# A two-layer streaming encoder: where the entry of gate and up keeps its norm scales, its rounded parts and its PSUM banks

## The chip, the core and the metric

The kernel runs on one core of one Trainium2 chip. The metric is the device time of one execution in microseconds, the median of several runs.

## The reference, cut to what matters

Two request groups (1024 prompt frames, and 8 x 16 sample frames) go through two trunk layers with width 1024. Each layer is a mixer with a residual and then a gated feed-forward block with a residual:

```python
h = rmsnorm(x, norm_mix[layer])
x = x + mixer(h)                    # layer 0: S5 + gated DeltaNet, then @ w_out; layer 1: windowed attention, then @ wo
x = x + swiglu(rmsnorm(x, norm_ffn[layer]), w_gate, w_up, w_down)

def rmsnorm(x, w):  y = x * rsqrt(mean(x * x) + 1e-6);  return y * w
def swiglu(h, w_gate, w_up, w_down):  return (silu(h @ w_gate) * (h @ w_up)) @ w_down
```

All is fp32. The change sits where each layer passes from the projection (`@ w_out` or `@ wo`) to the norm and to the products with `w_gate` and `w_up`.

## The kernel before, in words

The activations stand transposed: `x` is 8 chunks of 128 channels by 1152 frames, and the frames are cut in 3 blocks of 384 (`BW`). A product in fp32 is made of three matmuls on fp32r values (`mm3`, lines 436 to 438): each operand is split into a rounded part (`hi`, a ScalarE copy) and a remainder (`lo`, source minus `hi`, on VectorE).

`project` makes the projection. In its second half it goes over blocks and chunks; each of the 24 results is accumulated in one of two PSUM banks (`bank`), VectorE adds it into `x` (line 1509), ScalarE squares it (line 341), GpSimd adds up the squares (line 347), and after the eighth chunk of a block `rms` (lines 349 to 364) sums them over the partitions with matmuls into a bank `pn` and makes the scale 1/rms of the block in an SBUF tile `r`.

`ffn` follows. `scale` (line 478) multiplies the eight chunks of a block by the norm's weight and by the block's scale: 8 VectorE instructions, one block at a time, 24 for a layer. Gate and up are made by a fast algorithm of 20 products (`UP_A`, `UP_ORDER`) whose right operands are sums of quarters of the three blocks. `put` (lines 464 to 469) splits one such operand of 128 x 768: one ScalarE instruction for `hi`, one VectorE instruction for `lo`; 20 for a layer. The output tiles `f` = 0 and 1 (`g0`, `g1`) are worked on in turns while the operands are being made; tiles 2 to 21 follow with all operands ready. `weights` sums the weight quarters on GpSimd (line 518) and splits them (lines 522 and 523). Accumulators of `tile_of` go round `banks`: here one `bank` (2 buffers) and three `pa` (6 buffers), eight PSUM banks in all. They are evicted by `copy` (line 549, ScalarE) and `op` (line 555, mostly VectorE).

The order of instructions on each engine is made beforehand by a list scheduler from the order in the program, from priorities (`Sooner` moves evictions and splits forward) and from a model of costs; on the chip each engine goes through its list in order. `mphase` closes a layout of six PSUM banks and opens the next. The six `pa` banks are opened in `ffn`, after the whole projection; the norm sums of the projection use the layout before it.

Of the kernel before, what the change touches and what calls it, by code (L numbers as in the profile page):

```python
# [24 lines left out]
KC = 8  # L25
# [177 lines left out]
def body(tc, nc, I, O):  # L203
# [55 lines left out]

    class Sooner:  # L260
# [88 lines left out]
    def rms(r, b, parts, first=0):  # L349
# [13 lines left out]
        V.scalar_tensor_tensor(y, t, 1.5, y, ALU.add, ALU.mult)  # L363
# [5 lines left out]
    def norm(w, h, r, new, first, keep=None):  # L369
# [4 lines left out]
        def fill(x, k, b, i=None):  # L374
# [4 lines left out]
            if i == KC - 1:  # L379
                rms(r, b, parts, first)  # L380
# [64 lines left out]
    def ffn(x, pre, l, w, nxt):  # L445
        r, hb, c_hb, tp, c_tp, d_r = pre
# [3 lines left out]
        fp, c_fp = po.open(f"fa{l}", side="right")  # L450
        mphase(pa=6)
        banks = itertools.cycle([bank] + [lambda: mbank("pa")] * 3)

        def two(i):
            n = UP_ORDER.index(i)
            pool, tag, bufs = ((hp, "h", 4 * NB), (fp, "u", 4), (hb, "f", 4))[(n >= 12) + (n >= 16)]
# [5 lines left out]
        def put(i, t, neg=False):  # L462
            U[i] = hi, lo = two(i)
            if neg:
                S.activation(hi, t, AF.Copy, scale=-1.0)
                V.scalar_tensor_tensor(lo, t, -1.0, hi, ALU.mult, ALU.subtract)
            else:
                S.copy(hi, t)
                V.tensor_sub(lo, t, hi)  # L469
# [4 lines left out]
        def scale(t, order=range(4)):  # L474
            for q in order:
                for k in (2 * q, 2 * q + 1):
                    o = x[:, k, blk(UP_T[t])]
                    V.scalar_tensor_tensor(o, o, nw[:, w * KC + k:w * KC + k + 1], r[:, blk(UP_T[t])], ALU.mult, ALU.mult)
# [160 lines left out]

        scale(0)  # L640
        b0, b1, b2 = (quarter(t) for t in range(3))
        put(4, b0[3], True)
        put(10, b0[0], True)
        scale(2, (1, 0, 2, 3))
# [4 lines left out]
        V.tensor_add(b2[0], b0[0], b2[0])  # L649
        put(17, b2[0], True)  # L650
# [61 lines left out]
        finishing(g1)  # L712

# [798 lines left out]
    def project(name, ap, x, opnd, view, w, between, places=()):  # L1512
# [23 lines left out]
        between()  # L1536
        wb, c_wb = po.open(name)
# [4 lines left out]
        fill = norm(w, {}, r, lambda: wb.tile([128, BW], F32, name="sq", tag="sq", bufs=3), 0)  # L1542
# [12 lines left out]
        for b in range(NB):  # L1555
            for m in range(KC):
                def ev(b, s, p):
                    add_into(x, m)(b, s, p)
                    if m % 2:
                        Q.dma_start(d_r[m // 2][:, :, s], x.tiles[m // 2][:, :, s])  # L1560
                    fill(x, m, b)
                t = terms(W[m // 2], 512 * (m % 2), 1)
# [422 lines left out]
```

## Time and profile before

| | |
|---|---|
| median of 3 runs | 2755.37 us (2753.17 to 2763.01) |
| profiled execution | 2758.04 us, span 2756.3 us |
| mean granted TensorE clock | 0.960 of full speed |
| busy, share of the span | PE 94%, VectorE (DVE) 72%, ScalarE (ACT) 40%, GpSimd (POOL) 60% |

The span goes from the first to the last instruction. A busy time is the time in which an engine had an instruction in work; two that overlap are counted once. A duration is that of one instruction. A wait in brackets is the idle time of the engine ahead of the instruction, with the one that ended it.

### The profile page before, as it was taken

Reading aid. Unit: us, or ns where it says so; the run is one execution under the profiler, and the core shown is the slowest. Engines: PE = TensorE matmul, PEld = TensorE weight load, DVE = VectorE, ACT = ScalarE, POOL = GpSimd, SP = SyncE. Lnnn points to the kernel's source line nnn. Section 1 sums busy time; section 2 is a strip of 40 time slices with the busy share of each in tenths; the row PEclk is TensorE's granted clock in tenths of the full one; section 3 lists DMA queues with packets and bytes.
Section 4 is the critical chain, followed back from the end, with each engine's and each line's share of the span. In section 5 each row is a group of like instructions: output and inputs, shape, how many; then the busy total and the mean of one; then the engine's idle time right before and its main releaser. Section 6 shows DMA issues by size and latency. Waiting matters only on the chain.

```text
span 2756.3 us, 40229 instructions
## 1 busy us (share of the span) xinstructions
PE 2587.2 (94%) x14777; PEld 2404.8 (87%) x14777; DVE 1997.0 (72%) x3195; ACT 1109.8 (40%) x2232; POOL 1643.3 (60%) x1659
## 2 busy tenths in 40 slices
PE   6898899998799999989999999999789999989996
PEld 5788798997799999989998966667689999989996
DVE  7747874668878777698866245555978777789967
ACT  5234565444344434343333144343334443444332
POOL 8649432226598887897632012113688888788735
PEclk9899999999899999999999999798999999999998
DMA  6432277632022222253313100202122222253311
GB/s 204 134 102 87 95 240 220 189 131 87 33 102 78 91 72 80 79 186 98 98 32 110 61 16 24 86 29 85 33 99 78 77 89 75 74 175 105 100 54 69
DMA packets 164164, 267.20 MB, mean 97 GB/s; under 512 B 34188, under 2 KB 123948, under 8 KB 162928
## 3 DMA queue, kind: packets, MB, share of 16 engines
q1 hardware_dynamic: 163392, 262.28, 29.5%
q8 instruction: 116, 1.90, 0.3%
q10 hardware_dynamic: 576, 2.36, 0.2%
q14 instruction: 80, 0.66, 0.1%
HBM read 186.92 MB, written 79.51 MB: 97 GB/s over the span
## 4 chain that ended last, share of the span: by engine, by line
PE 67%; DVE 13%; POOL 11%; issue 3%; DMA 2%; ACT 2%; SPq 0%; DVEq 0%; POOLq 0%; ACTq 0%
PE pa L436 6%; PE pa L437 6%; PE pa L438 6%; PE pg L307 3%; PE pg L309 3%; PE pg L308 3%; PE pd L438 3%; PE pd L436 3%; PE pd L437 3%; PE b L436 3%; PE b L438 3%; PE b L437 3%; PE pO L1897 3%; PE pS L1870 2%; POOL x L518 2%
## 5 line engine op out<-in xcount | busy, mean ns | idle before, releaser
L436 PE MATMUL pa<-u,whi 128*128 128x384 f32 x928 | 319.6, 344 | 26.5 <-DVE bt L555 13.2
L438 PE MATMUL pa<-u,wlo 128*128 128x384 f32 x928 | 310.3, 344 | 11.3 <-DVE wlo L523 11.3
L437 PE MATMUL pa<-u,whi 128*128 128x384 f32 x928 | 317.2, 342 | 1.5 <-DVE u L469 1.2
L437 PE MATMUL pd<-g,whi 128*128 128x384 f32 x708 | 239.9, 339 | 0.0
L436 PE MATMUL pd<-g,whi 128*128 128x384 f32 x708 | 239.1, 338 | 0.5 <-ACT nt L810 0.5
L438 PE MATMUL pd<-g,wlo 128*128 128x384 f32 x708 | 237.7, 337 | 0.0
L523 DVE TENSOR_TENSOR wlo<-x,whi 128x1024 fp32r<-128x1024 f32 (+2 forms) x176 | 202.7, 1170 | 44.9 <-ACT whi L522 44.5
L522 ACT CAST whi<-x 128x1024 fp32r<-128x1024 f32 (+2 forms) x176 | 129.7, 761 | 256.0 <-PE pa L437 148.6
L1858 POOL TENSOR_SCALAR p<-p,rd 128x192 f32<-128x192 f32 (+3 forms) x80 | 61.3, 768 | 285.7 <-DVE rd L1852 181.0
L518 POOL TENSOR_TENSOR x<-raw 128x256 f32<-128x256 f32 (+1 forms) x230 | 209.9, 936 | 25.7 <-DMA raw<-in_wg_dram 14.7
L436 PEld LDWEIGHTS pa<-u,whi 128*128 128x128 f32 x928 | 178.7, 193 | 32.8 <-DVE bt L555 13.9
L518 POOL TENSOR_TENSOR cm<-raw 128x256 f32<-128x256 f32 (+1 forms) x162 | 158.9, 1002 | 60.3 <-DVE wlo L523 28.0
L438 PEld LDWEIGHTS pa<-u,wlo 128*128 128x128 f32 x928 | 178.7, 193 | 13.6 <-DVE wlo L523 13.6
L284 ACT CAST whi<-raw 128x1024 fp32r<-128x1024 f32 x113 | 116.5, 1049 | 182.7 <-PE pg L308 83.7
L285 DVE TENSOR_TENSOR wlo<-raw,whi 128x1024 fp32r<-128x1024 f32 x113 | 164.6, 1456 | 23.4 <-ACT whi L284 22.7
L437 PEld LDWEIGHTS pa<-u,whi 128*128 128x128 f32 x928 | 178.6, 192 | 2.8 <-DVE u L469 1.7
L436 PE MATMUL pa<-u,x 128*128 128x384 f32 x428 | 146.1, 341 | 4.4 <-DVE bt L555 4.0
L307 PE MATMUL pg<-h0h,whi 128*128 128x384 f32 x384 | 135.0, 352 | 12.1 <-DVE ut L949 11.4
L437 PE MATMUL pa<-u,x 128*128 128x384 f32 x428 | 145.5, 340 | 0.0
L518 POOL TENSOR_TENSOR x<-x 128x256 f32<-128x256 f32 (+1 forms) x142 | 129.2, 930 | 23.1 <-DVE wlo L523 16.4
L438 PE MATMUL pa<-u,x 128*128 128x384 f32 x428 | 141.9, 341 | 0.3
L772 DVE TENSOR_TENSOR g<-gf,g 128x384 fp32r<-128x384 f32 x132 | 135.4, 1052 | 4.3 <-ACT g L771 4.3
(731 smaller groups left out, 8112.6 us busy)
## 6 DMA issues: line engine op xcount, KB each, us to landing
gf<-d_g SPq DMA_DIRECT2D x44, 576.0 KB
raw<-in_wd_dram SPq DMA_DIRECT2D x44, 512.0 KB
raw<-in_wg_dram SPq DMA_DIRECT2D x28, 512.0 KB
raw<-in_wu_dram SPq DMA_DIRECT2D x28, 512.0 KB
raw<-in_win_dram SPq DMA_DIRECT2D x21, 512.0 KB
d_r<-x SPq DMA_DIRECT2D x24, 384.0 KB
x<-d_r SPq DMA_DIRECT2D x8, 1152.0 KB
x<-in_wg_dram SPq DMA_DIRECT2D x16, 512.0 KB
```

Of the source, the lines that this page charges most:

```text
L284: S.copy(hi, raw)
L285: V.tensor_sub(lo, raw, hi)
L307: PE.matmul(p[:, :BW], hi[:, c], rh, start=(i == 0), stop=False)
L308: PE.matmul(p[:, :BW], hi[:, c], rl, start=False, stop=False)
L309: PE.matmul(p[:, :BW], lo[:, c], rh, start=False, stop=(i == len(ks) - 1))
L436: PE.matmul(p, hi[:, c], uh, start=start, stop=False, skip_group_check=more)
L437: PE.matmul(p, hi[:, c], ul, start=False, stop=False, skip_group_check=more)
L438: PE.matmul(p, lo[:, c], uh, start=False, stop=stop, skip_group_check=more)
L518: (P.tensor_add if sg > 0 else P.tensor_sub)(cm[:, 256 * j:256 * (j + n)], fa, ga)
L522: S.copy(hi[:, c], src)
L523: V.tensor_sub(lo[:, c], src, hi[:, c])
L772: eng.tensor_sub(op[1], t, op[0])
```

## The change

Norm scales: `rms` may write the scale of a block into the PSUM bank `pn` that held its sum, and `scale` reads it there. Remainders: `split` takes the place of `put`'s two instructions; ScalarE makes two rounded copies of 128 x 384 in two PSUM banks `ph`, then `hi` of 128 x 768 in SBUF as before, and VectorE makes `lo` in two instructions of 128 x 384, each from the source in SBUF and a rounded copy in PSUM. Banks: one layout for projection and entry, `pn` 1, `ph` 2, `pa` 3, opened ahead of the projection's second half; the products of `f` = 0 and 1 go round five banks, and the six `pa` are opened for `f` = 2 and on. Since one `pn` bank now holds a scale until it is used, `project` becomes a generator, and `ffn` asks for its three blocks between its own first steps.

```diff
--- before.py
+++ after.py
@@ -257,6 +257,19 @@
 
         return behind(S.preload_act_table_set("natural_log_exp_and_others"), *others)
 
+    def split(hi, lo, src, neg=False):
+
+
+        p = [mbank("ph")[:, :BW].bitcast(F32R) for c in range(2)]
+        for c in range(2):
+            S.activation(p[c], src[:, c], AF.Copy, scale=-1.0 if neg else 1.0)
+        S.activation(hi, src, AF.Copy, scale=-1.0 if neg else 1.0)
+        for c in range(2):
+            if neg:
+                V.scalar_tensor_tensor(lo[:, c], src[:, c], -1.0, p[c], ALU.mult, ALU.subtract)
+            else:
+                V.tensor_sub(lo[:, c], src[:, c], p[c])
+
     class Sooner:
 
 
@@ -346,7 +359,8 @@
         else:
             P.tensor_add(ssq[:, s], ssq[:, s], sq)
 
-    def rms(r, b, parts, first=0):
+    def rms(r, b, parts, first=0, banks=None):
+
 
         s = blk(b)
         y, v = r[:, s], ssq[:, s]
@@ -360,13 +374,16 @@
         act.append(S.activation(y, y, AF.Exp, scale=-0.5))
         V.scalar_tensor_tensor(t, y, -0.5, v, ALU.mult, ALU.mult)
         V.tensor_mul(t, t, y)
-        V.scalar_tensor_tensor(y, t, 1.5, y, ALU.add, ALU.mult)
+        o = y
+        if banks is not None:
+            o = banks[b] = p
+        V.scalar_tensor_tensor(o, t, 1.5, y, ALU.add, ALU.mult)
         return act
 
     def new_r():
         return rp.tile([128, T], F32, name="r", tag="r", bufs=1)
 
-    def norm(w, h, r, new, first, keep=None):
+    def norm(w, h, r, new, first, keep=None, banks=None):
 
 
         parts = []
@@ -377,7 +394,7 @@
                 split_in(x, h, w, k, b)
             square_in(x, k, b, i, new, parts, keep)
             if i == KC - 1:
-                rms(r, b, parts, first)
+                rms(r, b, parts, first, banks)
 
         return fill
 
@@ -443,30 +460,26 @@
             pool.tile([128, 1024], F32R, name=t, tag=t, bufs=2)
 
     def ffn(x, pre, l, w, nxt):
-        r, hb, c_hb, tp, c_tp, d_r = pre
+        r, hb, c_hb, tp, c_tp, d_r, project_block, scales = pre
         d_g = dr.tile([NF, 128, T], F32, name=f"d_g{l}")
 
 
-        fp, c_fp = po.open(f"fa{l}", side="right")
-        mphase(pa=6)
-        banks = itertools.cycle([bank] + [lambda: mbank("pa")] * 3)
+        def bp():
+            return mbank("pa")
+
+        banks = itertools.cycle([bank, bp, bank, bp, bp])
 
         def two(i):
             n = UP_ORDER.index(i)
-            pool, tag, bufs = ((hp, "h", 4 * NB), (fp, "u", 4), (hb, "f", 4))[(n >= 12) + (n >= 16)]
+            pool, tag, bufs = (hp, "h", 4 * NB) if n < 12 else (fp, "u", 4) if n < 16 else (hb, "f", 4)
             t = pool.tile([128, 4, BW], F32R, name=f"u{i}", tag=tag, bufs=bufs)
             return t[:, 0:2], t[:, 2:4]
 
         U = {}
 
         def put(i, t, neg=False):
-            U[i] = hi, lo = two(i)
-            if neg:
-                S.activation(hi, t, AF.Copy, scale=-1.0)
-                V.scalar_tensor_tensor(lo, t, -1.0, hi, ALU.mult, ALU.subtract)
-            else:
-                S.copy(hi, t)
-                V.tensor_sub(lo, t, hi)
+            U[i] = two(i)
+            split(*U[i], t, neg)
 
         def quarter(t):
             return [x.tiles[q][:, :, blk(UP_T[t])] for q in range(4)]
@@ -475,7 +488,7 @@
             for q in order:
                 for k in (2 * q, 2 * q + 1):
                     o = x[:, k, blk(UP_T[t])]
-                    V.scalar_tensor_tensor(o, o, nw[:, w * KC + k:w * KC + k + 1], r[:, blk(UP_T[t])], ALU.mult, ALU.mult)
+                    V.scalar_tensor_tensor(o, o, nw[:, w * KC + k:w * KC + k + 1], scales[UP_T[t]], ALU.mult, ALU.mult)
 
         def some(name="bt", bufs=2):
             return tp.tile([128, 2, BW], F32, name=name, tag=name, bufs=bufs)
@@ -637,16 +650,20 @@
             for _ in g:
                 pass
 
+        next(project_block)
         scale(0)
         b0, b1, b2 = (quarter(t) for t in range(3))
         put(4, b0[3], True)
         put(10, b0[0], True)
+        next(project_block)
         scale(2, (1, 0, 2, 3))
         t13 = some("b13", 1)
         V.tensor_add(t13, b0[0], b2[1])
         put(13, t13)
         P.tensor_add(b0[1], b0[1], b2[1])
         V.tensor_add(b2[0], b0[0], b2[0])
+        next(project_block, None)
+        fp, c_fp = po.open(f"fa{l}", side="right")
         put(17, b2[0], True)
         put(16, b0[1], True)
         put(19, b2[1], True)
@@ -710,6 +727,8 @@
         put(9, b1[3], True)
         finishing(g0)
         finishing(g1)
+        mphase(pa=6)
+        banks = itertools.cycle([bank] + [bp] * 3)
 
 
         t, u = x.new(2, [128, 2 * T], F32R), x.new(3, [128, 2 * T])
@@ -1509,7 +1528,7 @@
             V.tensor_add(x[:, m, s], x[:, m, s], p[:, :BW])
         return f
 
-    def project(name, ap, x, opnd, view, w, between, places=()):
+    def project(name, ap, x, opnd, view, w, between, places=(), after=()):
 
 
 
@@ -1534,12 +1553,14 @@
                 for b in range(NB if m2 == 0 else NB - 1):
                     mm(b, m, terms(W, 512 * (m % 2), 0), add_into(x, m))
         between()
+        mphase(pn=1, ph=2, pa=3)
         wb, c_wb = po.open(name)
         W = [panel(ap[1, m2], p) for m2, p in enumerate((None, None) + (places or (wb, wb)))]
         hb, c_hb = po.open("hb", side="right")
         tp, c_tp = po.open("tp", side="right")
         r = new_r()
-        fill = norm(w, {}, r, lambda: wb.tile([128, BW], F32, name="sq", tag="sq", bufs=3), 0)
+        scales = {}
+        fill = norm(w, {}, r, lambda: wb.tile([128, BW], F32, name="sq", tag="sq", bufs=3), 0, banks=scales)
         d_r = dr.tile([KC // 2, 128, 2, T], F32, name=f"d_r{w}")
         again = {}
         for i in range(4):
@@ -1552,26 +1573,29 @@
                 hi, lo = again[m]
                 S.copy(hi, raw[:, blk(m % 2, 512)])
                 V.tensor_sub(lo, raw[:, blk(m % 2, 512)], hi)
-        for b in range(NB):
-            for m in range(KC):
-                def ev(b, s, p):
-                    add_into(x, m)(b, s, p)
-                    if m % 2:
-                        Q.dma_start(d_r[m // 2][:, :, s], x.tiles[m // 2][:, :, s])
-                    fill(x, m, b)
-                t = terms(W[m // 2], 512 * (m % 2), 1)
-                if b == NB - 1 and m > 1:
-                    t = terms(again[m], 0, 0) + t
-                mm(b, m, t, ev)
-        c_wb()
-        return r, hb, c_hb, tp, c_tp, d_r
+        def by_block():
+            for b in range(NB):
+                for m in range(KC):
+                    def ev(b, s, p):
+                        add_into(x, m)(b, s, p)
+                        if m % 2:
+                            Q.dma_start(d_r[m // 2][:, :, s], x.tiles[m // 2][:, :, s])
+                        fill(x, m, b)
+                    t = terms(W[m // 2], 512 * (m % 2), 1)
+                    if b == NB - 1 and m > 1:
+                        t = terms(again[m], 0, 0) + t
+                    mm(b, m, t, ev)
+                if b == NB - 1:
+                    c_wb()
+                    for c in after:
+                        c()
+                yield
+
+        return r, hb, c_hb, tp, c_tp, d_r, by_block(), scales
 
     pre = project("wb0", I["wout"], x, lambda b, k: mixo[b][k], lambda p: p, 1, c_g2,
                   (tuple(ybuf("w")[:, :1024].bitcast(F32R) for _ in range(2)),
-                   tuple(gt.tile([128, 1024], F32, name="w", tag="TT", bufs=2).bitcast(F32R) for _ in range(2))))
-    c_gt()
-    c_y5()
-    c_L0()
+                   tuple(gt.tile([128, 1024], F32, name="w", tag="TT", bufs=2).bitcast(F32R) for _ in range(2))), (c_gt, c_y5, c_L0))
 
     nxt = {}
 
@@ -1966,7 +1990,6 @@
     def between():
         c_wk()
         c_qp()
-        env["mphase"](m=2)
 
     return x, c_x, project("wb1", I["wo"], x, lambda b, k: tuple(t[:, :, k % 4, :] for t in oT[b][k // 4]),
                            lambda p: p.rearrange("p (c k) -> p c k", c=6), 3, between)
```

## Rows read from the trace of the kernel before

**Rows 1.** The page: busy time of the engines, and the granted clock in 40 slices.

```profile
PE 2587.2 (94%) x14777; PEld 2404.8 (87%) x14777; DVE 1997.0 (72%) x3195; ACT 1109.8 (40%) x2232; POOL 1643.3 (60%) x1659
...
PEclk9899999999899999999999999798999999999998
```

**Rows 2.** Stretches, entry of layer 0: length, busy by engine (instructions), clock, DMA.

```profile
640.00:648.00 8.00, 4.24 (x20) 2.99 (x18) 7.96 (x11) 0.72 (x2) 5.17 (x5) 0.96 0.09 33
648.00:660.00 12.00, 11.71 (x50) 11.44 (x51) 6.64 (x11) 5.31 (x9) 4.43 (x6) 0.74 0.19 67
660.00:669.80 9.80, 6.61 (x39) 6.29 (x37) 9.77 (x12) 1.54 (x2) 5.42 (x3) 1.00 0.37 108
669.80:690.00 20.20, 16.75 (x81) 16.13 (x82) 18.15 (x16) 8.48 (x14) 14.79 (x8) 0.87 0.11 40
690.00:699.00 9.00, 9.00 (x36) 7.77 (x35) 4.47 (x7) 1.73 (x4) 2.56 (x2) 0.71 0.12 44
699.00:707.70 8.70, 4.21 (x25) 3.89 (x23) 8.70 (x11) 2.67 (x5) 4.26 (x2) 0.87 0.00 1
707.70:742.00 34.30, 26.63 (x106) 23.43 (x106) 33.64 (x45) 14.71 (x27) 20.02 (x17) 0.78 0.08 22
742.00:760.00 18.00, 15.38 (x73) 13.91 (x73) 10.97 (x14) 6.07 (x9) 13.58 (x14) 0.91 0.17 62
sum 120.00, PE 94.53 PEld 85.85 DVE 100.30 ACT 41.24 POOL 70.22; mean PE 11.82 PEld 10.73 DVE 12.54 ACT 5.15 POOL 8.78
```

**Rows 3.** The same view, entry of layer 1 (1904.9 to 2028.2 us), its sum.

```profile
sum 123.30, PE 96.69 PEld 89.58 DVE 101.99 ACT 42.97 POOL 71.76; mean PE 12.09 PEld 11.20 DVE 12.75 ACT 5.37 POOL 8.97
```

**Rows 4.** The same stretches, line 478 alone: DVE busy; last, layer 1's sum.

```profile
640.00:648.00 8.00, 6.80 (x8) 0.96 0.09 33
...
660.00:669.80 9.80, 8.11 (x8) 1.00 0.37 108
...
699.00:707.70 8.70, 7.45 (x8) 0.87 0.00 1
...
sum 123.30, DVE 22.47; mean DVE 2.81
```

**Rows 5.** The same stretches: line 466 alone (two rows), then line 469 alone.

```profile
669.80:690.00 20.20, 6.60 (x4) 0.87 0.11 40
...
707.70:742.00 34.30, 2.35 (x1) 0.78 0.08 22
...
669.80:690.00 20.20, 5.57 (x4) 0.87 0.11 40
...
707.70:742.00 34.30, 9.23 (x7) 0.78 0.08 22
```

**Rows 6.** Lines 478, 1509, 1174, 361: instructions, ns min/median/max.

```profile
L478 DVE SCALAR_TENSOR_TENSOR x<-x,nw,r x48: 602/608/2208, 640.6 to 1972.2; 128x384 f32<-128x384 f32 x48
...
L1509 DVE TENSOR_TENSOR x<-x,pg x84: 536/551/557, 520.0 to 1958.4; 128x384 f32<-128x384 f32 x84
...
L1174 DVE SCALAR_TENSOR_TENSOR A<-pS,CT,Dm x36: 333/341/346, 213.0 to 355.7; 128x128 f32<-128x128 f32 x36
...
L361 DVE SCALAR_TENSOR_TENSOR nt<-r,ssq x15: 530/558/1391, 24.1 to 2745.5; 128x384 f32<-128x384 f32 x15
```

**Rows 7.** Timeline of DVE: four evictions in a row, start and time.

```profile
748.88 1.94 DVE L555 TENSOR_TENSOR x<-x,pa 128x384 f32<-128x384 f32 x4
```

**Rows 8.** Timeline of PE in the entry of layer 0, with idle time ahead.

```profile
707.77 0.69 PE L438 MATMUL pa<-u,wlo 128*128 128x384 f32 x1 [4.55 <-DVE wlo L523]
...
717.15 0.44 PE L436 MATMUL pa<-u,whi 128*128 128x384 f32 x1 [1.36 <-ACT u L468]
...
728.33 0.44 PE L436 MATMUL pa<-u,u 128*128 128x384 f32 x1 [2.66 <-DVE x L555]
```

**Rows 9.** ACT: squares of 128 x 384 (line 341) and `hi` of 128 x 768.

```profile
L341 ACT ACTIVATE sq<-x 128x384 f32<-128x384 f32 x42 | 21.3, 520 | 44.8 <-DVE x L1509 42.0 <-issue 2.5 <-POOL ssq L347 0.3
...
L468 ACT CAST u<-x x12: 815/830/834, 673.6 to 2019.1; 128x768 fp32r<-128x768 f32 x12
```

## Prediction

> **What bounds the kernel now.** I read the page first. TensorE (PE) is busy for 94% of the span, so time can be won only where PE stands idle or runs at less than its full clock [rows 1]. The slices show the granted clock at nine tenths or more nearly everywhere, so such places are few; two of them are the passages from projection to gate and up. I then cut the passage of layer 0 into stretches at the points where PE stopped [rows 2]. [...] The passage of layer 1 has the same form: 123.30 us with 96.69 busy, 26.6 idle [rows 3]. The reader should look at the column of VectorE (DVE) beside that of PE: in each stretch in which PE is idle, DVE is full or nearly so (7.96 of 8.00, 9.77 of 9.80, 18.15 of 20.20, 8.70 of 8.70, 33.64 of 34.30). DVE sets the pace here. ScalarE (ACT) has 41.24 us of the 120 in use and GpSimd (POOL) 70.22.
>
> The lines of DVE that the change touches come next. The 24 scale instructions of line 478 come in three batches of 8, which take 6.80, 8.11 and 7.45 us, 22.4 in all, and 22.47 in layer 1 [rows 4]. One of them takes 602 ns at best, and 2208 at worst [rows 6]. The remainders (lines 466 and 469) take 6.60 + 5.57 = 12.17 us for 8 in the stretch to 690 us and 2.35 + 9.23 = 11.58 for 8 in the one to 742 us [rows 5]; the other four are few and early or late.
>
> **What the PSUM operands do.** The durations say when DVE is slow. Line 361 has both tensors in SBUF, and varies from 530 to 1391 ns; line 478 is of the same kind. Line 1509 has one tensor in SBUF and one in PSUM, and none of its 84 instances is above 557 [rows 6], though many ran in these same stretches beside a busy POOL. So what stretches the others is two SBUF inputs while POOL works, and one operand in PSUM takes that away. Line 478 also reads a weight for each partition from SBUF. Line 1174 has just that mix (PSUM tensor, weight for each partition, SBUF tensor), and its 36 stay within 333 to 346 ns at 128 columns [rows 6]. I take it that the weight does no harm.
>
> Prices. Four evictions in a row take 1.94 us [rows 7]; with 0.54 for the last, they are (1.94 - 0.54) / 3 = 0.47 apart. A remainder becomes two such instructions: 0.94. A scale instruction takes 0.61 at its best, and 0.07 of it lies under the next one, as with the evictions (0.54 against 0.47), so 0.54 apart and 4.3 for a batch. If the price were instead the full 0.61, a batch would be 4.9; if the wait stayed, it would be as now.
>
> [...] The trace has PSUM operands (line 1509, median 551 ns) no dearer than SBUF operands without a wait (line 361, 530 at best, 558 at the median) [rows 6]. [...]
>
> **The change part by part**, for layer 0, in the order of the stretches. What a batch saves counts only up to PE's idle time in its stretch.
>
> - To 648 us: the first batch, 6.80 - 4.3 = 2.5; PE is idle for 3.8. Counts 2.5.
> - 660 to 669.8: the second batch, 8.11 - 4.3 = 3.8; PE idle 3.2. Counts 3.2.
> - 669.8 to 690: eight remainders, 12.17 - 7.5 = 4.7; PE idle 3.45. ACT gets sixteen more copies here. No row has ACT writing PSUM; the nearest, the squares of the same size, are 0.52 [rows 9], so 8.3 us on top of its 8.48, in 20.2. ACT becomes nearly as full as DVE. Bounds 0 and 3.45; I take 2.5, since ACT still fits.
> - 699 to 707.7: the third batch, 7.45 - 4.3 = 3.1; PE idle 4.5, most of it the one wait of 4.55 on a split queued behind the batch [rows 8]. Counts 3.1.
> - 707.7 to 742: eight remainders, 11.58 - 7.5 = 4.1; PE idle 7.7. Counts 4.1.
> - Elsewhere four remainders, where DVE has room: 0. Should that room go, they are worth about 1 us.
>
> Together 15.4. Against it:
>
> - `hi` now stands behind two copies on ACT, two times 0.45 later. PE waits for a `hi` in a few places, as 1.36 us at 717 [rows 8]; I count three, 2.7. Bounds 0, where the scheduler has the copies done early, and 2.7.
> - Five banks instead of eight. An accumulator of 6 to 18 matmuls takes 1 to 3 us, so four others give its eviction 4 us or more, where one eviction takes 0.54. But in a stretch in which DVE is full an eviction queues: PE waited 2.66 us for one at 728 with eight banks [rows 8]. Bounds 0 and 11 (each of the 20 accumulators one eviction later); I take 2, by the row of an uncrowded eviction.
> - [...] The stretches behind the stops ran at 0.74 and 0.71; bounds 0 and 6 (26% of 12 us and 29% of 9 us); I take 2.
>
> Nothing is counted for: the extra ACT work elsewhere, which lies under ACT's idle two thirds (if that goes, an eviction waits for up to 0.9); the weight loads and the stores of `x`, which keep their order on SP's queue; the layout opened early and changed again for `f` = 2, where the banks of the entry have long been read (a wait there would be one eviction, 0.54); the last instruction of `rms`, which still reads two SBUF tensors. The single `pn` bank makes the norm sum of the second block wait for the first batch of scales; that sum runs at about 656, the batch ends at 648.
>
> So 15.4 - 2.7 - 2 + 2 = 12.7 for a layer, 25 for both. The profiled execution took 2758.0 us (its span and 1.7 around it), which gives 2733; the median of the runs lies 2.7 lower. I predict 2730.
>
> **The rivals.**
>
> *ACT takes DVE's place* in the two stretches of remainders. There are two `ph` banks, so ACT's next pair of copies waits until DVE has read the last pair, and whatever stands behind them in ACT's list (weight splits, squares, evictions) waits too. If those stretches (2.5 and 4.1) yield nothing and the clock neither, 8.8 - 2.7 - 2 = 4.1 a layer, 8 in all: 2747 by the median. For it: 8.48 + 8.3 of 20.2 us. Against it: ACT's 14.71 of 34.30 in the longer stretch.
>
> *Five banks stall PE: slower.* PE's list has no other work when the next accumulator's bank is still to be evicted by a DVE that is working through a batch. Without the bank term a layer gains 14.7, which is used up when each of the 20 accumulators waits 0.74 us; at 1.2 us each a layer loses 9.3, and the time is 2774. For it: the 2.66 us wait with eight banks. Against it: DVE's batches, behind which evictions queue, get 40% shorter.
>
> *The scale instructions still wait on POOL*, since `x` and the weight both come from SBUF. Then the three batches (8.8) give nothing, and 6.6 - 2.7 - 2 leaves 2 a layer: 2751. Against it: line 1174.
>
> **How the numbers follow.** Forecast 0.68, ACT 0.16, banks 0.12, scales 0.04. A change of 0.5% (14 us) is about what measurement can tell from none. The forecast's own range: with the full 0.61 and 0.54 x 2 as prices (1.8 a layer less) and 5 for banks it ends at 2740; with all DVE time saved (9.5 for the batches, 9.8 for the remainders a layer), no loss and a clock gain of 4, at 2709. Both middle rivals (2747, 2751) belong in the range, which I end at no change, 2756; the bank rival and a little below 2709 stay out. Faster 0.68; same 0.20 (ACT and scales); slower 0.12.
>
> **What would show it right or wrong.** Line 478 at 0.60 to 0.62 us throughout, batches of 4.3 to 5; remainders at 0.54 to 0.56; each passage about 12 us shorter, PE's idle time near 13 instead of 25.5; ACT busy near 60 us of the passage. The forecast fails if PE waits mainly for evictions or for `hi` (banks, ACT), if line 478 keeps a spread above 0.7, or if the scheduler's list, made anew, costs time outside the two passages; that the rest stays within 3 us is assumed.

## The result, and the profile after

Five runs of each kernel, taken in turn on one chip, have their median at 2723.40 us after the change (2722.01 to 2726.89) and at 2756.42 us before it; the ratio is 0.9876, with a 95% interval of 0.9863 to 0.9890. That is 33 us less, where 25 were forecast (2730). The forecast's mechanism held; the sizes that it gave to three side effects did not, and that is what most of the experiments are about.

The page of the changed kernel, its busy times and the granted clock, answers to [rows 1]:

```profile
PE 2570.6 (94%) x14777; PEld 2387.2 (88%) x14777; DVE 1971.9 (72%) x3235; ACT 1144.7 (42%) x2312; POOL 1625.9 (60%) x1659
...
PEclk9999999999999999999999999798999999989998
```

PE has as many instructions as before, DVE has 40 more (two short remainders for each long one) and yet 25 us less of busy time, and ACT has 80 more, the copies into PSUM. In the clock's line the eleventh slice, in which most of the entry of layer 0 lies, shows a 9 where it showed an 8; slices of 68 us are too coarse for more, and the windows below are the place to look.

A passage means, from here on, the stretch from the first scale instruction of a layer to the first product whose weights lie in a tile of `x`; PE has the same matmuls in it in every kernel, but for five at most (and 30 added ones in one experiment). Its two windows (length, busy time by engine with instructions, clock, DMA), first before the change, where they are nearly the stretches of [rows 2, 3]:

```profile
640.58:759.98 119.40, 93.93 (x420) 85.25 (x418) 99.73 (x120) 41.22 (x67) 69.62 (x54) 0.84 0.13 42
1904.95:2028.23 123.28, 96.69 (x453) 89.59 (x453) 101.96 (x123) 43.00 (x70) 71.74 (x56) 0.88 0.14 46
```

and after it:

```profile
641.52:740.30 98.78, 81.93 (x421) 75.21 (x420) 86.87 (x140) 58.05 (x107) 60.15 (x54) 0.97 0.15 51
1888.24:1993.10 104.86, 89.49 (x453) 82.45 (x453) 87.02 (x143) 59.98 (x110) 61.13 (x56) 0.95 0.16 55
```

The passages are 20.6 and 18.4 us shorter, 39.0 together. Four columns matter. PE's idle time (length less busy) goes from 25.5 and 26.6 to 16.9 and 15.4. PE's busy time for the same matmuls falls by 12.0 and 7.2, with the clock, which goes from 0.84 and 0.88 to 0.97 and 0.95. DVE is busy for 12.9 and 14.9 us less. That is not all that its changed instructions save, 17.1 and 17.6 us: the 19 instructions of a passage that make the weights' remainders (lines 523 and 536), which read two SBUF tensors, take 18.7 and 18.1 us after the change instead of 15.8 and 15.7. POOL, whose work was not touched, is busy for 9.5 and 10.6 less with the same 54 and 56 instructions. The rest of the program is 2513.6 us before (2756.3 less both passages) and 2518.0 after, 4 more.

The instructions that the change made (count, shortest, median and longest in ns, first and last start), against [rows 6, 9]; of the remainders and the copies these are the commonest operands, the others (`bt`, `b`) last about as long:

```profile
L491 DVE SCALAR_TENSOR_TENSOR x<-x,nw,pn x48: 602/608/617, 641.5 to 1946.1; 128x384 f32<-128x384 f32 x48
```

```profile
L269 DVE SCALAR_TENSOR_TENSOR u<-x,ph x24: 541/548/555, 647.1 to 1986.9; 128x384 fp32r<-128x384 f32 x24
```

```profile
L271 DVE TENSOR_TENSOR u<-x,ph x24: 540/542/555, 677.4 to 1985.5; 128x384 fp32r<-128x384 f32 x24
```

```profile
L265 ACT ACTIVATE ph<-x x48: 469/483/502, 645.8 to 1986.2; 128x384 fp32r<-128x384 f32 x48
```

No scale instruction takes more than 617 ns (before: up to 2208), no remainder more than 555.

What PE waited for in the passage of layer 0 (sum in us, times, longest) is best read before and after. Before:

```profile
PE pg L1522 <- DVE x L1509: 7.1, 4, 3.2
PE pa L438 <- DVE wlo L523: 4.8, 2, 4.6
PE b L436 <- DVE x L1509: 2.8, 1, 2.8
PE pa L436 <- DVE x L555: 2.7, 1, 2.7
PE pa L436 <- ACT u L468: 2.0, 2, 1.4
PE pa L436 <- ACT x L549: 1.8, 1, 1.8
```

After:

```profile
PE pa L453 <- ACT whi L535: 3.9, 3, 2.3
PE pa L455 <- DVE wlo L536: 3.2, 1, 3.2
PE b L455 <- DVE wlo L536: 2.1, 1, 2.1
PE pg L1541 <- DVE x L1528: 2.1, 2, 1.7
PE b L453 <- DVE r L568: 1.8, 1, 1.8
PE b L453 <- ACT u L266: 1.5, 2, 0.9
```

The first and third line of before are the projection's evictions, which stood behind other work in DVE's list: 9.9 us, and 2.1 after. In layer 1 they were 9.2 and 2.2, and are 3.2. These evictions alone are 16 of the 20 us of idle time that went; other waits changed places, and the one for `whi`, the rounded part of a weight, grew to 3.9. The work ahead of the evictions was of both kinds that the change shortens. Of the 9.9 us, 6.4 (8.5 of 11.4 in layer 1) stood behind the norm and the batches of scales, the rest behind long remainders, as here in PE's and in DVE's timeline before (start, duration, idle time ahead and its end):

```profile
689.03 0.66 PE L436 MATMUL b<-u,whi 128*128 128x384 f32 x1 [2.76 <-DVE x L1509]
```

```profile
685.86 2.56 DVE L466 SCALAR_TENSOR_TENSOR u<-bt,u 128x768 fp32r<-128x768 f32 x1
```

The eviction in question starts at 688.34, right behind that remainder. After the change none of these waits is behind a remainder. At about the places of the stops of [rows 8] PE's timeline now has:

```profile
695.45 0.44 PE L455 MATMUL pa<-u,wlo 128*128 128x384 f32 x1 [3.22 <-DVE wlo L536]
...
703.76 0.44 PE L453 MATMUL b<-u,whi 128*128 128x384 f32 x1 [0.86 <-ACT u L266]
...
727.83 0.44 PE L453 MATMUL pa<-u,whi 128*128 128x384 f32 x1 [2.27 <-ACT whi L535]
```

### The profile page after: what moved, and what is told of

The parts are those of the page before. It is cut to its first block, busy times and chain, and to the rows that moved or that the text cites. A ratio compares the mean times of both kernels' runs of the same rounds, so it can differ in the third digit from the quotient of the medians.

```text
span 2721.6 us, 40367 instructions
## 1 busy us (share of the span) xinstructions
PE 2570.6 (94%) x14777; PEld 2387.2 (88%) x14777; DVE 1971.9 (72%) x3235; ACT 1144.7 (42%) x2312; POOL 1625.9 (60%) x1659
## 4 chain that ended last, share of the span: by engine, by line
PE 70%; DVE 12%; POOL 10%; issue 3%; DMA 3%; ACT 1%; SPq 0%; DVEq 0%; POOLq 0%; ACTq 0%
PE pa L454 6%; PE pa L453 6%; PE pa L455 6%; PE pd L453 4%; PE pd L455 4%; PE pd L454 4%; PE pg L320 3%; PE pg L322 3%; PE pg L321 3%; PE b L453 3%; PE b L455 3%; PE b L454 3%; PE pO L1921 3%; PE pS L1894 2%; PE pg L1541 2%
## 5 line engine op out<-in xcount | busy, mean ns | idle before, releaser
L453 PE MATMUL pa<-u,whi 128*128 128x384 f32 x904 | 306.9, 340 | 20.6 <-DVE bt L568 13.3
L455 PE MATMUL pa<-u,wlo 128*128 128x384 f32 x904 | 299.2, 339 | 9.8 <-DVE wlo L536 9.8
L454 PE MATMUL pa<-u,whi 128*128 128x384 f32 x904 | 305.3, 338 | 1.2 <-DVE u L269 1.1
L453 PEld LDWEIGHTS pa<-u,whi 128*128 128x128 f32 x904 | 171.3, 190 | 25.5 <-DVE bt L568 13.9
L531 POOL TENSOR_TENSOR cm<-raw 128x256 f32<-128x256 f32 (+1 forms) x162 | 153.2, 967 | 56.1 <-DVE wlo L536 19.7
L455 PEld LDWEIGHTS pa<-u,wlo 128*128 128x128 f32 x904 | 170.9, 190 | 11.5 <-DVE wlo L536 11.5
L298 DVE TENSOR_TENSOR wlo<-raw,whi 128x1024 fp32r<-128x1024 f32 x113 | 162.6, 1439 | 23.7 <-ACT whi L297 23.2
L454 PEld LDWEIGHTS pa<-u,whi 128*128 128x128 f32 x904 | 171.3, 190 | 2.2 <-DVE u L269 1.7
L320 PE MATMUL pg<-h0h,whi 128*128 128x384 f32 x384 | 135.7, 353 | 12.3 <-DVE ut L968 11.4
```

What stands on the lines that cost most here:

```text
L298: V.tensor_sub(lo, raw, hi)
L320: PE.matmul(p[:, :BW], hi[:, c], rh, start=(i == 0), stop=False)
L453: PE.matmul(p, hi[:, c], uh, start=start, stop=False, skip_group_check=more)
L454: PE.matmul(p, hi[:, c], ul, start=False, stop=False, skip_group_check=more)
L455: PE.matmul(p, lo[:, c], uh, start=False, stop=stop, skip_group_check=more)
L531: (P.tensor_add if sg > 0 else P.tensor_sub)(cm[:, 256 * j:256 * (j + n)], fa, ga)
```

## The experiments

Each of the twelve was timed beside the kernel before on one chip (4 to 12 runs of it). This table has their ratios, and from each one's profile the passages with PE's idle time, DVE's busy time and the granted clock in them, and what remains of the span.

| kernel | median us | ratio (95%) | layer 0: length, idle, DVE, clock | layer 1: length, idle, DVE, clock | rest |
|---|---|---|---|---|---|
| before | 2756.42 | 1 | 119.4, 25.5, 99.7, 0.84 | 123.3, 26.6, 102.0, 0.88 | 2513.6 |
| after | 2723.40 | 0.9876 (0.9863–0.9890) | 98.8, 16.9, 86.9, 0.97 | 104.9, 15.4, 87.0, 0.95 | 2518.0 |
| again | 2724.41 | 0.9875 (0.9855–0.9896) | 101.3, 14.9, 86.7, 0.92 | 105.0, 15.7, 87.0, 0.95 | 2522.0 |
| banks_only | 2758.97 | 1.0009 (0.9999–1.0018) | 114.7, 25.6, 100.8, 0.90 | 123.0, 26.9, 101.2, 0.89 | 2521.0 |
| scales_only | 2740.45 | 0.9938 (0.9924–0.9951) | 108.8, 19.9, 92.3, 0.89 | 115.1, 21.0, 93.8, 0.90 | 2518.5 |
| splits_only | 2742.25 | 0.9947 (0.9934–0.9960) | 108.0, 20.0, 93.4, 0.91 | 116.8, 23.2, 95.3, 0.90 | 2515.7 |
| hi_first | 2723.46 | 0.9885 (0.9870–0.9900) | 98.9, 15.7, 86.6, 0.97 | 103.4, 15.3, 86.9, 0.97 | 2516.3 |
| four_banks | 2718.81 | 0.9872 (0.9858–0.9886) | 97.0, 15.3, 86.8, 0.98 | 105.1, 15.6, 87.6, 0.95 | 2518.6 |
| banks_warm | 2756.94 | 1.0007 (0.9996–1.0018) | 115.7, 24.1, 100.3, 0.94 | 123.8, 24.9, 103.0, 0.92 | 2518.8 |
| twice | 2729.39 | 0.9892 (0.9877–0.9907) | 103.7, 18.5, 94.1, 0.93 | 107.8, 16.7, 95.5, 0.92 | 2518.6 |
| burst | 2734.20 | 0.9912 (0.9896–0.9929) | 106.8, 19.7, 99.8, 0.87 | 108.9, 18.3, 97.9, 0.91 | 2518.8 |
| tail_psum | 2723.69 | 0.9888 (0.9874–0.9902) | 98.9, 16.7, 86.9, 0.97 | 105.0, 15.4, 87.0, 0.95 | 2522.0 |
| tail_pd | 2726.12 | 0.9881 (0.9866–0.9896) | 98.7, 17.0, 86.9, 0.97 | 103.4, 15.9, 86.9, 0.97 | 2521.6 |
| best | 2728.33 | 0.9886 (0.9869–0.9902) | 100.0, 16.5, 85.9, 0.95 | 103.9, 14.5, 86.0, 0.93 | 2523.1 |

The medians of different rows come from several chips, whose kernel before had its median between 2755.1 and 2759.6; so the ratios are to be compared, not the medians. The row `again` is the changed kernel a second time. One profile stands behind each row's windows, and profiles differ where the program does not: the stretch ahead of the first passage, in which all engines have the same instructions in the same order in every kernel, ends between 639.9 and 645.8 us.

**banks_only.** The new layout of the banks and the projection driven block by block, with scales in SBUF and the old `put` (the edits here and below are against the changed kernel and abridged):

```
-            U[i] = two(i)
-            split(*U[i], t, neg)
+            U[i] = hi, lo = two(i)
+            S.copy(hi, t); V.tensor_sub(lo, t, hi)      # neg: as before
-        scales = {}
-        fill = norm(..., 0, banks=scales)
+        scales = {b: r[:, blk(b)] for b in range(NB)}
+        fill = norm(..., 0)
```

> Layout alone: norm scales in SBUF and one-copy remainders as before, but the projection in three steps, the layout pn 1, ph 2 (unused), pa 3 opened early, and five banks for tiles 0 and 1. If five banks cost 2 us a layer and early banks give nothing (the prediction's term), about 2760 us. If the gain of the change comes from products that can start before the projection ends, 2735 to 2745.

The layout is no gain by itself; the time is the same within 0.2%, as the expectation of 2760 had it. In its profile the passage of layer 0 is 4.7 us shorter, the rest 7 longer: 4.5 of the 7 lie between that passage and the attention, 2.2 in the attention, whose instructions stand in another order than before. That is so too in scales_only, splits_only, banks_warm, four_banks, twice and best, while the changed kernel keeps nearly the old order there, which bears on their times and not on their passages.

**scales_only.** As above, but with `banks=scales` kept: only the scales are in PSUM.

> Norm scales in PSUM, remainders made as before from the copy in SBUF. [...] If the remainders were the main part, 2745 or more.

**splits_only.** The changed kernel with the two lines of `scales` as in banks_only: only the remainders are made from PSUM.

> Remainders from rounded parts in PSUM, norm scales in SBUF as before. By the prediction's terms (6.6 a layer, less 2.7 for a later hi and 2 for banks) 2752; line 478's batches stay at 6 to 9 us. With a gain of clock of its own, 2740 to 2745.

Each half takes its share away from the same program: 0.71% beyond the layout for the scales, 0.62% for the remainders, 1.33% together, against 1.33% for both at once (1.0009 - 0.9876). So they add up in time, within intervals of 0.3%. In the passages they do not quite: scales_only has 13.8 us less than banks_only in the two, splits_only 12.9, 26.7 together, while both at once have 34.0 (31.4 in again). scales_only (2740.45) came where the prediction's terms put it: 8.8 for the batches less 2 for the banks are 6.8 a layer, which from 2755.37 gives 2742. splits_only missed its 2752 and came within 2740 to 2745, which was set down for a gain of clock of its own; its clock in the passages is 0.91 and 0.90, against 0.90 and 0.89. The instructions show that each edit mends its own kind and leaves the other as it was. In scales_only, the scale and one kind of remainder:

```profile
L496 DVE SCALAR_TENSOR_TENSOR x<-x,nw,pn x48: 600/608/615, 644.9 to 1959.2; 128x384 f32<-128x384 f32 x48
```

```profile
L484 DVE SCALAR_TENSOR_TENSOR u<-x,u x12: 946/1398/1767, 650.6 to 2007.7; 128x768 fp32r<-128x768 f32 x12
```

and in splits_only the scale:

```profile
L491 DVE SCALAR_TENSOR_TENSOR x<-x,nw,r x48: 604/613/2208, 644.0 to 1962.3; 128x384 f32<-128x384 f32 x48
```

**hi_first.** In `split`, the copy that PE reads goes ahead of the two that DVE reads:

```
         p = [mbank("ph")[:, :BW].bitcast(F32R) for c in range(2)]
+        S.activation(hi, src, AF.Copy, scale=...)
         for c in range(2):
             S.activation(p[c], src[:, c], AF.Copy, scale=...)
-        S.activation(hi, src, AF.Copy, scale=...)
```

> As changed, but ScalarE makes hi of 128 x 768 first and the two rounded copies after it. If TensorE's waits for hi cost 2.7 us a layer, 2718; the remainders start 0.8 us later each. If the order of the three does not matter, 2723 within 3 us; if the remainders are the more urgent, above 2726.

No difference from the changed kernel: 0.9885 against 0.9876, with intervals that overlap, and passages of 98.9 and 103.4. The 2.7 us a layer that the prediction took off were not there.

**four_banks.**

```
-        mphase(pn=1, ph=2, pa=3)
+        mphase(pn=1, ph=2, pa=2)
```

> The changed kernel with one bank fewer: the first two tiles of gate and up share four banks in turn instead of five (`pa` two instead of three). The prediction charged the step from eight banks to five with 2 us a layer, because an eviction would have to queue behind DVE's batches. If that price is real, the step from five to four costs at least as much again: 2 us or more a layer, 2728 or more. Rival: an accumulator of 1 to 3 us of matmuls always finds a bank that was evicted long before, the banks cost nothing at five or at four, and the time stays at 2721 to 2726; then the 2 us of the prediction belonged to nothing.

Even four banks cost nothing (0.9872; 97.0 and 105.1 us). The 2 us a layer for the step from eight to five were not there either.

**banks_warm.** Does the clock count by itself? To banks_only, whose entry still waits as before, this adds matmuls that nobody reads, at two stops:

```
+        FILL = {(0, 3): 12, (1, 18): 18}
+        def warm(n, w, u, last):
+            if n:
+                d = mbank("ph")[:, :BW]
+                for j in range(n):
+                    last = behind(PE.matmul(d, w[0][:, blk(0, 128)], u[0][:, 0], start=True, stop=True), last)
...
+                    last = prod(p, W, i, ...)
+                    warm(FILL.get((f, i), 0), W[i], U[i], last)
```

> The kernel with the new layout alone, and 30 matmuls of no use in each layer's entry (written to the two `ph` banks that this kernel leaves empty, read by nobody): 12 after the product of the fourth block difference of tile 0, 18 after the one before it of tile 1, which is where PE stood still for 3.7 and 4.1 us and ran on at 0.32 us a matmul. DVE's and ACT's work is as it was. The passages of the layout alone took 114.7 and 123.0 us. If the granted clock is a term by itself, the full clock behind these two stops gives back most of (0.32 - 0.17) x about 40 matmuls, 4 to 6 us a layer: passages of about 109 and 118. Rival: DVE sets the end of these stretches, PE at its full clock only reaches the next stop sooner, and the passages stay within 2 us of 114.7 and 123.0 (or grow by the useless matmuls that overrun a stop). The passages are to be read, not the whole time: the order in the attention comes out differently too.

The windows of banks_only and then of this kernel:

```profile
641.60:756.33 114.73, 89.11 (x422) 81.01 (x420) 100.80 (x120) 41.33 (x67) 70.53 (x54) 0.90 0.13 44
1907.96:2030.92 122.96, 96.05 (x452) 88.49 (x452) 101.23 (x123) 42.98 (x70) 70.86 (x56) 0.89 0.14 47
```

```profile
639.94:755.60 115.66, 91.55 (x452) 83.77 (x451) 100.31 (x120) 41.36 (x67) 68.69 (x53) 0.94 0.13 44
1903.89:2027.64 123.75, 98.83 (x482) 90.62 (x483) 103.01 (x123) 42.87 (x70) 71.52 (x56) 0.92 0.14 46
```

The clock rises from 0.90 to 0.94 and from 0.89 to 0.92, and the passages do not get shorter (115.7 and 123.8). The rival holds: a PE that runs faster here reaches its next wait sooner. PE's timeline in layer 0 shows it, first of banks_only, then of banks_warm:

```profile
698.22 0.69 PE L453 MATMUL pa<-u,whi 128*128 128x384 f32 x1 [2.71 <-ACT whi L540]
...
706.17 0.69 PE L455 MATMUL pa<-u,wlo 128*128 128x384 f32 x1 [3.74 <-DVE wlo L541]
```

```profile
694.84 2.26 PE L551 MATMUL ph<-u,u 128*128 128x384 f32 x12
...
697.75 0.44 PE L453 MATMUL pa<-u,whi 128*128 128x384 f32 x1 [0.65 <-ACT whi L541]
...
705.70 0.69 PE L455 MATMUL pa<-u,wlo 128*128 128x384 f32 x1 [5.57 <-DVE wlo L542]
```

The first twelve useless matmuls fill the stop of 2.71 us down to 0.65, and the next stop, for the remainder of a weight, grows from 3.74 to 5.57: what was won is waited for one step later. The weight's remainder comes when DVE makes it, and PE's clock has no part in that. Over a passage the useless matmuls take 5.6 and 5.5 us, the others 3.2 and 2.7 less than in banks_only, and the idle time goes down by 1.5 and 2.0 only. The test is a partial one: behind the stop of 5.57 us the matmuls start 0.32 us apart until 708.4, and 0.17 to 0.18 from then on, so the slower pace is not gone from the passage.

**twice.** DVE's work put back, in another shape: the first half of each remainder is made twice, to the same place.

```
                 V.tensor_sub(lo[:, c], src[:, c], p[c])
+            if c == 0:      # and the same for neg
+                V.tensor_sub(lo[:, c], src[:, c], p[c])
```

> The changed kernel with 20 DVE instructions more in each layer's entry: the remainder of the first half of each of the 20 operands is made twice, to the same place. Nothing is added to PE, ACT or POOL. They are 0.47 us apart, so 9.4 us of DVE a layer. If DVE sets the length of the entry, the passages of 98.8 and 104.9 us grow by nearly all of it, to about 108 and 114, and the time to about 2740. Rival: PE and its clock set it, and DVE's idle time (11.9 of 98.8, 17.8 of 104.9) takes the extra work up: passages within 3 us, 2723 to 2729.

Between the two: DVE is busy for 7.2 and 8.4 us more, and the passages grow by 4.9 and 2.9 against the profile of after (2.5 and 2.8 against that of again). So a passage does not follow DVE's busy time one to one.

**burst.** The same amount, but in the batches of scales, seven of eight products written once more to a place that nobody reads:

```
                     o = x[:, k, blk(UP_T[t])]
+                    if k < 7:
+                        V.scalar_tensor_tensor(r[:, blk(UP_T[t])], o, nw[...], scales[UP_T[t]], ALU.mult, ALU.mult)
                     V.scalar_tensor_tensor(o, o, nw[...], scales[UP_T[t]], ALU.mult, ALU.mult)
```

> The changed kernel with 21 DVE instructions more in each layer's entry, now inside the three batches of scales: seven of the eight products of each batch are also written to a place that nobody reads. They are about 0.5 us apart, so 10 to 11 us of DVE a layer, as much as the batches have lost by the change, and at the same place. The kernel with 20 remainders made twice had nearly the same amount spread over the operands, and its passages grew by 4.9 and 2.9 us only. If it is DVE work in front of PE's waits that counts, the passages grow by 8 to 11 us a layer here, to about 108 and 114, and the time to 2740 or more. Rival: only the amount of DVE work counts and much of it is taken up by idle time: 3 to 6 us a layer, 2730 to 2735.

```profile
642.55:749.37 106.82, 87.08 (x419) 78.71 (x418) 99.79 (x161) 57.99 (x107) 57.47 (x54) 0.87 0.14 47
1896.61:2005.49 108.88, 90.61 (x453) 83.88 (x453) 97.94 (x164) 59.89 (x110) 60.47 (x56) 0.91 0.16 53
```

The passages grow by 8.0 and 4.0 us (5.6 and 3.9 against the profile of again), the time by 0.37% against again on the same chip (about 10 us). That is what the rival had (2730 to 2735); the 2740 or more that work in front of PE's waits was to cost did not come. This row is the most telling of all: DVE is as busy as it was before the change (99.8 and 97.9, against 99.7 and 102.0), and the passages are still 12.6 and 14.4 us shorter. Three differences stand out. The same amount lies elsewhere, with the batches at 27.0 us instead of 22.4 and the remainders at 20.5 and 20.7 instead of 28.3 and 28.6. POOL is busy for 57.5 and 60.5 instead of 69.6 and 71.7. And the evictions no longer stand behind a whole batch. DVE's timeline at the entry of layer 1, before:

```profile
1904.95 6.29 DVE L478 SCALAR_TENSOR_TENSOR x<-x,nw,r 128x384 f32<-128x384 f32 x8
1911.17 1.00 DVE L1509 TENSOR_TENSOR x<-x,pg 128x384 f32<-128x384 f32 x2
```

in the changed kernel, with the same order:

```profile
1888.24 4.28 DVE L491 SCALAR_TENSOR_TENSOR x<-x,nw,pn 128x384 f32<-128x384 f32 x8
1892.44 1.01 DVE L1528 TENSOR_TENSOR x<-x,pg 128x384 f32<-128x384 f32 x2
```

and in burst:

```profile
1896.61 0.61 DVE L492 SCALAR_TENSOR_TENSOR r<-x,nw,pn 128x384 f32<-128x384 f32 x1
1897.25 0.61 DVE L493 SCALAR_TENSOR_TENSOR x<-x,nw,pn 128x384 f32<-128x384 f32 x1
1897.78 0.61 DVE L492 SCALAR_TENSOR_TENSOR r<-x,nw,pn 128x384 f32<-128x384 f32 x1
1898.31 0.55 DVE L1530 TENSOR_TENSOR x<-x,pg 128x384 f32<-128x384 f32 x1
```

The scheduler, which orders the list when the kernel is built, has here put an eviction after every few scale instructions; PE waits 0.9 and 0.4 us for them in the two passages, where it waited 9.9 and 11.4 before and 2.1 and 3.2 in the changed kernel. Work that the scheduler counts on can be arranged for; for the time that instructions lost on the chip, the list of before shows no such arrangement. Since burst changes the amount of work, its place and the order at once, how much belongs to each is not separated.

**tail_psum, tail_pd and best.** The same idea for the final norm, whose last batches of five are on the chain that ends last. First with a bank taken from the down projection, then with one of its five in turn, then that and a third `ph` bank:

```
-            rms(r, b, parts)
+            sc = mbank("pd")[:, :BW]          # tail_pd, best; tail_psum: banks=sc, pd=4, pn=2
+            rms(r, b, parts, scale_bank=sc)
...
-                        V.scalar_tensor_tensor(x[:, i, s], x[:, i, s], wk, r[:, s], ALU.mult, ALU.mult)
+                        V.scalar_tensor_tensor(x[:, i, s], x[:, i, s], wk, sc, ALU.mult, ALU.mult)
```

> The changed kernel, and the same idea used once more: the scale of the final norm stays in a PSUM bank (the down projection has four banks of its own instead of five), so that the last 24 scale instructions read one tensor from SBUF and one from PSUM. In the changed kernel the last batches of five take 5.43, 5.05 and 4.94 us beside a busy POOL, on the chain that ends last. If they wait on POOL as line 478 did, they go to about 2.7 each, and 5 to 7 us of the end go: about 2717. Rival: the fifth bank of the down projection is worth as much as the batches, or the stores behind the batches set the end, and the time is 2722 or more.

> The changed kernel with the final norm's scale in PSUM again, now in one of the five banks of the down projection, which keeps all five; the copy in SBUF for POOL's three multiplications is made by one more DVE instruction. The kernel with four banks there had its three last batches at 2.71 us instead of 5.43, 5.05 and 4.94, and yet the time did not move: its first batch began 9.4 us later than in the changed kernel. If the bank taken from the down projection (and the copy on ACT ahead of the batches, 0.55 to 0.60 a batch) cost that, this kernel has the batches' 5 to 7 us: 2717 to 2719. Rival: the end is set by POOL's three multiplications and the stores, and the time stays at 2722 to 2725.

> The final norm's scale in a bank of the down projection, and four banks in turn for tiles 0 and 1, the freed bank being a third one for the rounded parts (`ph`). ACT stood for 7.7 us in all before copies into `ph` that DVE had still to read. If these waits hold DVE up, another 1 to 3 us go, and the two together give 2714 to 2717; if DVE is full anyway, the third bank gives nothing and the time is that of the final norm's change alone.

DVE's timeline at the end, in the changed kernel and in tail_pd:

```profile
2696.42 5.43 DVE L1636 SCALAR_TENSOR_TENSOR x<-x,nw,r 128x384 f32<-128x384 f32 x5
...
2705.28 5.05 DVE L1636 SCALAR_TENSOR_TENSOR x<-x,nw,r 128x384 f32<-128x384 f32 x5
...
2712.69 4.94 DVE L1636 SCALAR_TENSOR_TENSOR x<-x,nw,r 128x384 f32<-128x384 f32 x5
```

```profile
2702.92 0.56 DVE L373 TENSOR_SCALAR ssq<-pn 128x384 f32<-128x384 f32 x1 [5.58 <-ACT r L372]
...
2706.12 2.71 DVE L1639 SCALAR_TENSOR_TENSOR x<-x,nw,pd 128x384 f32<-128x384 f32 x5
...
2715.76 2.70 DVE L1639 SCALAR_TENSOR_TENSOR x<-x,nw,pd 128x384 f32<-128x384 f32 x5
```

The batches take half as long, as expected, and the time does not move (0.9888, 0.9881 and 0.9886, all with the changed kernel's 0.9876 inside their intervals): DVE now stands idle for 5.58 us, until the norm's sum has passed through POOL, PE and ACT. The gain became a wait for work ahead of it, which the scheduler put in another order. In tail_psum the first of the three batches at the end begins at 2705.8, where it began at 2696.4. Behind the passage of layer 1 the profiles have 727.0 us in tail_psum, 734.5 in tail_pd and 736.6 in best, against 728.5 in the changed kernel. So all three expectations of a gain (2714 to 2719) were missed, and the times are those of the rivals. Nothing faster than the changed kernel came out; four_banks, at 0.9872, cannot be told from it.

**again.**

> The changed kernel as it is, once more, beside the one above on the same chip: its passages are expected within 1.5 us of 98.8 and 104.9, and what the stretch between the two passages and the rest of the program vary by from one profile to the next says how much of the 4 us lost outside the passages can be taken for a loss.

The passage of layer 0 is 101.3 in this profile, 2.5 longer than in the first (1.5 at most was expected), with the clock at 0.92 instead of 0.97. PE's matmuls take 4.4 us more; 2.0 of them come out of its idle time, and 2.5 lengthen the passage. The order of the instructions is the same, and DVE's timeline shows one place where the slower matmuls are felt, the wait for one of the projection's last sums, in the first profile and then in this one:

```profile
674.31 0.56 DVE L1528 TENSOR_TENSOR x<-x,pg 128x384 f32<-128x384 f32 x1 [0.39 <-PE pg L1543]
```

```profile
680.16 0.56 DVE L1528 TENSOR_TENSOR x<-x,pg 128x384 f32<-128x384 f32 x1 [1.67 <-PE pg L1543]
```

There DVE waits for PE, and a lower clock costs time; in the stretches of banks_warm PE waits for DVE. The rest of the program is 2522.0 against 2518.0. So two profiles of one program differ by 4 us there.

## Why the prediction was right, and where its sizes were off

- *The price of a scale batch*, 4.3 us: right. Batches take 4.28 and 4.29; the 24 instructions of layer 0 take 12.95 instead of 22.36. The rival that they still wait on POOL falls: none above 617 ns, though `x` and the weight come from SBUF, while the last instruction of `rms`, which still reads two SBUF tensors, takes up to 1266.
- *The price of a remainder*, two instructions 0.47 apart: right (0.54 to 0.56 each). All remainders of a passage take 20.6 us instead of 28.3 and 28.6. That is 7.7 to 8.0 saved, where 9.8 was the most that the prediction allowed for.
- *PSUM operands no dearer than SBUF operands without a wait*: right. The scale's minimum is 602 ns, and its median 608, with the operand in SBUF and in PSUM alike.
- *What a batch saves counts up to PE's idle time in its stretch*: the sum with that cap was 15.4 a layer, 10.7 after the charges for `hi` and the banks, and PE's idle time fell by 8.6 and 11.2. But the passages fell by 20.6 and 18.4, because PE's busy time fell too, by 12.0 and 7.2. Before the change PE was not only idle, it ran part of its matmuls at a slower pace (in layer 0 they start 0.32 us apart from 648.8 to 654.2, behind the stop that ends at 648.3, and 0.17 to 0.18 from then to 655.8), and in banks_warm running them faster only lengthened a later wait. One reading is that PE's slack in a stretch in which another engine sets the pace is its idle time and what its matmuls take longer than at full clock; by it the cap was too strict. It is argued and not shown, all the more since the layout may have a part: against banks_only the passages fell by 15.9 and 18.1.
- *`hi` behind two copies*, minus 2.7: nothing (hi_first). The remaining waits for `hi` in layer 0 are 1.5 us (0.9 in hi_first), where 2.2 stood before.
- *Five banks*, minus 2: nothing (four_banks). For the evictions of gate and up in layer 0 PE waited 2.7 and 1.8 us before, and 1.8 after.
- *The clock*, plus 2 and at most 6, counted in the change's favour for shorter stops of PE: the term that is furthest off, for PE's busy time fell by 12.0 and 7.2, with the clock of the passages at 0.97 and 0.95 instead of 0.84 and 0.88. No run shows this term by itself, and what it is worth is not settled. In banks_warm a higher clock (0.94 and 0.92, against 0.90 and 0.89) without the shorter waits gained nothing; between the two profiles of the changed kernel the passage of layer 0 was 2.5 us longer at the lower one (0.92 against 0.97).
- *The rest within 3 us*: not held in the profiles, +4 and +8. The gain in time (33.0) is also less than the 39.0 and 36.4 of the passages in the two profiles. In banks_only the passages yield 5.0 and the time nothing. Some 3 to 6 us are lost outside the passages. In the first profile 3.0 of the 4 lie between the two passages, in the second 5.2 of the 8 lie ahead of the first one; with 4 us between two profiles of one program, and one profile of the kernel before, their place is not settled.
- *The rivals*: ACT is busy for 58.1 and 60.0 us, near the 60 foretold, and did not take DVE's place (1.5 us of waits for `u`). The banks did not stall PE.
- *The range*: with the full prices the prediction's own stretches give 2.3 a layer less, where it has 1.8. The upper end of 2740 becomes 2741, and nothing hangs on it.

So the mechanism was right, and the terms were mis-sized. PE's idle time was to fall by 10.7 a layer and fell by 8.6 and 11.2, though `hi` and the banks, which had been charged with 4.7 of it, cost nothing. The clock was to bring 2, and PE's busy time fell by 12.0 and 7.2. Outside the passages, which were put at nothing, 2 to 3 a layer came back. Together that is 16.5 a layer where 12.7 were forecast; that the total came so near is in part luck, since errors of both signs lie in it.

What is shown and what is not: that the two edits act each by itself, and add up in time, is shown. That shorter waits for the projection's evictions made up 16 of the 20 us of idle time that PE lost is read from the waits. burst gives back 12.0 of the 39.0 us of the passages. How the other 27.0 divide between the shorter remainders, POOL's 9.5 to 10.6 us, which feed the weight splits, and the order of the evictions, was not told apart.

## What to carry to other kernels

Price an instruction that stalls on another engine by its shortest instance (602 ns for the scale instruction here; none took more than 617 after the change, where the worst had taken 2208), and count its whole saving where other work stands queued behind it. Cap that saving by the other engine's slack, which by the reading above, argued and not shown, may be more than its idle time when its clock is low there: with PE's clock at 0.84 and 0.88 before, its idle time fell by 8.6 and 11.2 us and the passages by 20.6 and 18.4. Side effects that are booked at "a few waits of this kind" deserve a look at how often the list has that work ready early: here two of them were nothing. And what a busy-time column gives back when the same amount of work is added again tells whether it was the amount or the place and the stalls that counted.

## What was not expected of the hardware

- The stall has two sides. POOL's 54 instructions of the passage of layer 0 took 69.6 us before and 60.2 after without being touched, and 61.2 in splits_only, 67.4 in scales_only: by this the long remainders cost it most.
- A PSUM output did not help. The last instruction of `rms` still reads two SBUF tensors and now writes PSUM; its six instances (same columns as above) spread as the old ones did, which took 0.56 to 1.25 us:

```profile
L380 DVE SCALAR_TENSOR_TENSOR pn<-nt,r x6: 695/1120/1266, 640.2 to 1941.7; 128x384 f32<-128x384 f32 x6
```

- ACT copies 384 columns from SBUF to PSUM in 483 ns at the median, no more than its squares of the same size to SBUF take (520 on average, [rows 9]); the functions differ, so the place of the output is not singled out.
- A PE that is kept busy with matmuls of no use had a higher clock over the passage (0.94 instead of 0.90 in layer 0), and it gained nothing in that passage, where DVE is busy for 100.3 of the 115.7 us (114.7 without those matmuls).
